# The distance bias of the second stage, written to DRAM in 16 transfers instead of 4, from a tile of its own

## The chip, the cores and the metric

The kernel runs on one core of one Trainium2 chip. Its time is the device time of one execution in microseconds (us); the number that counts is the median of several executions. The engines are TensorE (PE in the profile, its weight loads PEld), VectorE (DVE), ScalarE (ACT), GpSimd (POOL) and SyncE (SP). ACT and SP also issue DMAs: ACTq and SPq are such issues.

## What is computed

The program is one token mixer block with a large expert layer (the first block), followed by two hybrid layers (the second stage), for 256 tokens of width 1024 in float32. Cut to the parts that matter here:

```python
def first_block(...):
    h = rmsnorm(x, g_mix[l]);  proj = h @ w_in[l]
    attn_out = windowed_gqa(q_a, k_a, v_a, attn_sink[l])
    lru_out = bidir_rglru(xc, ...) * jax.nn.gelu(gate_l)
    mem_out = memory_cross_attention(q_m, k_m, v_m)
    g = jax.nn.sigmoid(gates + gate_b[l])
    merged = g0 * (attn_out @ p_attn) + g1 * (lru_out @ p_lru) + g2 * (mem_out @ p_mem)
    x = x + merged @ w_out[l]
    x = x + peer_ffn(rmsnorm(x, g_ffn[l]), ...)

def swa_attention(...):            # in each of the two layers of the second stage
    dist = qi - kj
    bias = rel_bias[t5_bucket(jnp.maximum(dist, 0))]      # 8 heads, a row of 384 distances each
    s = jnp.where(valid, s + bias, -jnp.inf)
```

The bias depends on the distance between two tokens alone. So one row of 384 numbers per head says all of it, and a tile of 128 queries needs that row 128 times, each time shifted by one place.

## The kernel before

**Weights.** All weights lie in DRAM in the order in which they are used, in pieces of 1 MB (16 blocks of 128x128). `Stream._slot` (line 76) loads a piece into one of two `raw` buffers (line 86, issued by SP), and for each half of it, a slot of 8 blocks, ACT writes the high part `whi` (line 90) and DVE the rest `wlo` (line 93). There are three `whi`/`wlo` buffers. Each product is three matmuls (`mm3`, lines 173 to 175; `mm3a`, lines 179 to 181). So a weight piece can be loaded once both slots of the piece two before it have been split.

**The order of the work.** The first block, `block1`, runs its projections one after the other on PE. What is not a projection (convolution, attention heads, the recurrence `lru`) is written as generators, which `add` puts into a list; `tick`, called for every second weight block, steps those that are due. A `yield n` makes a task wait `n * 4` ticks, which is `n * 8` weight blocks. `finish` runs a task to its end at once. The framework's scheduler then sets the order on each engine. Each engine works strictly in its order.

**The bias.** `rel_bias` (line 1428) is such a task, added in line 448. It loads the 32x8 table and a 33x384 one-hot matrix `boh`, multiplies them (line 1438, `prb`), copies the 8x384 result to SBUF (line 1440, `sbb`), and writes that to the DRAM scratch `bias_scr` 128 times, once for each query row, in four transfers of 32 copies (lines 1442 to 1446), issued by ACT. Each transfer reads 8 partitions and writes 8x32 pieces of 384 floats (1536 bytes). `issue_after(ws.on_scalar)` only says that the issue stands behind the latest `whi` on ACT. Each transfer is followed by `yield 2`. `self.finish(t_rel)` stands in line 594, ahead of the gated projections. The scratch is read much later, in the second stage (`bias`, line 1096).

**Tiles that share a place.** `sbb` has the tag `b2`, with three buffers, which it shares with `boh`, with `pts` of the attention (line 666) and with `lth` of the recurrence (line 549). A new tile of a tag waits until the tile three before it has been read by all its readers. For `sbb` the readers are the four transfers.

**What comes after.** The gated projections (`gated`, line 608) are 8 columns each for three branches: `pg` on PE, `gth` on ACT (line 617), `pp` on PE. The recurrence `lru` is finished inside them. Then come the output projection (line 604) and the expert layer, which begins with a transfer of `keys` (line 934, issued by ACT).

Of the kernel before, what the change touches and what calls it, by code (L numbers as in the profile page):

```python
# [7 lines left out]
F32 = mybir.dt.float32  # L8
# [11 lines left out]
P = 128  # L20
# [28 lines left out]
N_WARM = 50  # L49
NORM_AT = (5, 6)  # L50
REL_AT = 20
LOAD_AT = (2, 2, 4, 6, 10, 12, 12, 14, 14)


# [71 lines left out]
def blocks(*tiles):  # L126
    return [t[:, i, :] for t in tiles for i in range(t.shape[1])]


class Core:  # L130
# [285 lines left out]
    def block1(self):  # L416
        tc, nc, a, ws = self.tc, self.nc, self.a, self.ws
        with ExitStack() as st:
# [3 lines left out]
            p = st.enter_context(tc.tile_pool(name="b1", bufs=1))  # L422
# [4 lines left out]
            def T6(dt=F32):  # L427
                return pa.tile([P, 6, S], dt, tag="t6", name="t6", bufs=8)
# [4 lines left out]
            def raw16():  # L433
                b = blocks(T6(F32R), T6(F32R), T6(F32R))
                return [(b[i], b[8 + i]) for i in range(8)]
# [7 lines left out]
            with tc.issue_after(last[0].ins), tc.issue_after(last[1].ins):  # L443
# [3 lines left out]
                self.small1(p)  # L447
            t_rel = self.add(self.rel_bias(p), REL_AT)

# [141 lines left out]
                                          oh[:, h, :], ol[:, h, :]), 2 + 2 * h) for h in range(4)]  # L591


            self.finish(t_rel)
            mg = p.tile([P, KD, S], F32, tag="x8", name="mg", bufs=1)
            gh, gl_ = T8(), T8()
            br = [(0, "p_attn", 6, ah, al, t_att), (2, "p_mem", 4, oh, ol, t_mem), (1, "p_lru", 6, lh, ll, [t_lru])]
# [2 lines left out]
                           self.hgb[:, n * KD:n * KD + KD], b == 0, b == len(br) - 1, ts)  # L600
            self.dump("mg", mg)

            raw = raw16()
            acc = self.residual(("w_out", 0, 0), KD, gh, gl_, raw, self.pc("g_ffn"))
            self.lead(("w_peer_q", 0, 0), raw, self.pc("g_ffn"), [acc], lambda ps: self.rsqrt(ps[:, 0, :]), LEAD_Q)
# [459 lines left out]
    def mixers(self, l):  # L1065
        tc, nc, a, ws = self.tc, self.nc, self.a, self.ws
        with ExitStack() as st:
# [25 lines left out]
            def load(out, in_):  # L1093

                with tc.issue_after(ws.on_scalar):
                    nc.scalar.dma_start(out=out, in_=in_)
                return
                yield
            loads = [[self.add(load(o, i), w) for w, o, i in x] for x in (
                [(LOAD_AT[0], sink, a["swa_sinks"][l].to_broadcast([P, 8]))]  # L1100
                + [(LOAD_AT[1 + i], bias[:, 4 * i:4 * i + 4, :],
                    bass.AP(scr.tensor, scr.offset + 127 + 4 * 384 * i, [[8 * 384 - 1, P], [384, 4], [1, S]]))
                   for i in range(2)],
                [(LOAD_AT[3], cl[:, :L_DEC], a["cstl"][:, :L_DEC])],
                [(LOAD_AT[4], cl[:, L_DEC:], a["cstl"][:, L_DEC:])],
                [(LOAD_AT[5], wst, a["gmlp_wsT"][l]), (LOAD_AT[6], bs, a["gmlp_bs"][l].to_broadcast([P, 512])),
                 (LOAD_AT[7], lng[:, 0, :], a["gmlp_ln_g"][l].to_broadcast([P, 512])),
                 (LOAD_AT[8], lng[:, 1, :], a["gmlp_ln_b"][l].to_broadcast([P, 512]))])]
# [319 lines left out]
    def rel_bias(self, p):  # L1428

        nc, a = self.nc, self.a  # L1430
        rb = p.tile([33, 8], F32, tag="rlb", name="rlb")
        nc.vector.memset(rb, NEG)
        nc.scalar.dma_start(out=rb[0:32, :], in_=a["rel_bias"])
        oh = p.tile([33, 384], F32, tag="b2", name="boh", bufs=3)
        nc.scalar.dma_start(out=oh, in_=a["bucket"])
        self.bias_scr = self.dr.tile([P, 8 * 384], F32, name="bias_scr")
        ps = self.bg.tile([8, 384], F32, tag="bg", name="prb")
        nc.tensor.matmul(ps, lhsT=rb, rhs=oh, start=True, stop=True)
        sb = p.tile([8, 384], F32, tag="b2", name="sbb", bufs=3)
        nc.scalar.activation(out=sb, in_=ps, func=AF.Copy)  # L1440
        scr = self.bias_scr
        for i in range(0, P, 32):
            with self.tc.issue_after(self.ws.on_scalar):
                nc.scalar.dma_start(out=bass.AP(scr.tensor, scr.offset + i * 8 * 384, [[384, 8], [8 * 384, 32], [1, 384]]),
                                    in_=sb[:, None, :].to_broadcast([8, 32, 384]))
            yield 2

    def ffn(self, l):
        tc, nc, a, ws = self.tc, self.nc, self.a, self.ws
# [173 lines left out]
```

## Time and profile before

| | us |
|---|---|
| median of 3 executions | 2127.13 (2122.9 to 2136.53) |
| the profiled execution | 2123.62 |
| its span, first to last instruction | 2121.8 |
| PE busy in the span | 2032.5 (96%) |
| ACT busy in the span | 1164.8 (55%) |

The profile shows one execution. Matmuls overlap in the records, so a row's length is longer than the distance to the next one's start; the distance is what a matmul costs. A row "ACTq ... DMA_DIRECT2D" or "SPq ..." is the issue of a transfer, in which the issuing engine is held; the transfer itself runs on the core's 16 DMA engines, and "landing" is the time from issue to its arrival. An entry "[3.78 <-ACT whi L90]" is idle time of that engine just before the instruction, and what ended it.

### The profile page before, as it was taken

To read this page: it belongs to the slowest core of one execution; us is meant where nothing else is said; L and a number is where in the kernel's file an instruction comes from. 1 tells how busy PE (TensorE), PEld (TensorE's weight loads), DVE (VectorE), ACT (ScalarE), POOL (GpSimd) and SP (SyncE) were. 2 spreads that over 40 slices of the span, in tenths; PEclk is the share of its full clock that TensorE was granted. 3 is DMA by queue.
4 is the path that set the end of the run, shared out by engine and by line. 5 is a ranking of instruction groups with operands and counts; after the bars stand their busy time and mean duration, and the time that the engine had idled before them with its cause. 6 is when DMAs were issued, how large, how long until landed. Compare 5 with 4: busy or idle time off the path is not lost.

```text
span 2121.8 us, 41452 instructions
## 1 busy us (share of the span) xinstructions
PE 2032.5 (96%) x16818; PEld 1974.2 (93%) x16818; DVE 1680.1 (79%) x3308; ACT 1164.8 (55%) x1910; POOL 252.3 (12%) x162
## 2 busy tenths in 40 slices
PE   8978999959999999999999989999999999999999
PEld 7958999959999899999999878999999988999997
DVE  7847669998999999996556998977655898977654
ACT  6648754435555455554446656466545657466543
POOL 2101205844000000000000110210000110200000
PEclk9988999979999999999999999999999999999999
DMA  5443554525445444444555642555555643554554
GB/s 209 147 119 124 181 210 168 179 100 178 173 171 177 151 168 179 177 177 163 197 193 185 217 159 100 185 196 178 208 191 197 236 159 120 187 191 179 199 194 154
DMA packets 56923, 370.01 MB, mean 174 GB/s; under 512 B 6491, under 2 KB 10140, under 8 KB 13468
## 3 DMA queue, kind: packets, MB, share of 16 engines
q1 hardware_dynamic: 50256, 357.06, 46.9%
q10 hardware_dynamic: 6476, 10.31, 1.9%
q8 instruction: 131, 2.15, 0.4%
q14 instruction: 60, 0.49, 0.1%
HBM read 364.73 MB, written 2.62 MB: 173 GB/s over the span
## 4 chain that ended last, share of the span: by engine, by line
PE 81%; DVE 9%; issue 3%; DMA 3%; ACT 3%; POOL 1%; ACTq 0%; SPq 0%; POOLq 0%; DVEq 0%
PE mm L175 6%; PE mm L173 6%; PE mm L174 6%; PE acc L174 5%; PE pu L173 5%; PE acc L175 5%; PE acc L173 5%; PE pu L175 5%; PE pu L174 5%; PE pg L175 3%; PE pg L174 3%; PE pg L173 3%; DVE wlo L93 2%; PE mml L173 2%; PE mml L175 2%
## 5 line engine op out<-in xcount | busy, mean ns | idle before, releaser
L90 ACT ACTIVATE whi<-raw 128x1024 fp32r<-128x1024 f32 x677 | 716.9, 1060 | 764.6 <-PE acc L174 170.3
L93 DVE TENSOR_TENSOR wlo<-raw,whi 128x1024 fp32r<-128x1024 f32 x629 | 778.3, 1238 | 323.6 <-ACT whi L90 320.7
L173 PE MATMUL pu<-hh,whi 128*128 128x256 f32 x1024 | 290.5, 284 | 20.3 <-ACT whi L90 20.3
L175 PE MATMUL pu<-hh,wlo 128*128 128x256 f32 x1024 | 287.0, 280 | 3.1 <-POOL wlo L93 3.1
L174 PE MATMUL pu<-hl,whi 128*128 128x256 f32 x1024 | 286.1, 279 | 0.0
L175 PE MATMUL mm<-hh,wlo 128*128 128x256 f32 x1008 | 280.8, 279 | 5.3 <-DVE wlo L93 5.3
L173 PE MATMUL mm<-hh,whi 128*128 128x256 f32 x1008 | 281.6, 280 | 0.0
L174 PE MATMUL mm<-hl,whi 128*128 128x256 f32 x1008 | 280.3, 278 | 0.0
L174 PE MATMUL acc<-ga,whi 128*128 128x256 f32 x1000 | 267.9, 280 | 4.5 <-DVE ga L187 4.4
L175 PE MATMUL acc<-ga,wlo 128*128 128x256 f32 x1000 | 267.3, 279 | 0.0
L173 PE MATMUL acc<-ga,whi 128*128 128x256 f32 x1000 | 242.5, 281 | 5.0 <-ACT ga L186 5.0
L173 PEld LDWEIGHTS pu<-hh,whi 128*128 128x128 f32 x1024 | 194.7, 190 | 20.5 <-ACT whi L90 20.5
L173 PE MATMUL pg<-hh,whi 128*128 128x256 f32 x704 | 199.5, 283 | 12.3 <-ACT lth L552 11.7
L175 PE MATMUL pg<-hh,wlo 128*128 128x256 f32 x704 | 198.4, 282 | 0.6 <-DVE wlo L93 0.5
L175 PEld LDWEIGHTS pu<-hh,wlo 128*128 128x128 f32 x1024 | 194.3, 190 | 3.8 <-POOL wlo L93 3.8
L174 PE MATMUL pg<-hl,whi 128*128 128x256 f32 x704 | 197.7, 281 | 0.0
L175 PEld LDWEIGHTS mm<-hh,wlo 128*128 128x128 f32 x1008 | 190.3, 189 | 7.8 <-DVE wlo L93 6.7
L174 PEld LDWEIGHTS pu<-hl,whi 128*128 128x128 f32 x1024 | 194.0, 189 | 0.0
L174 PEld LDWEIGHTS acc<-ga,whi 128*128 128x128 f32 x1000 | 188.6, 189 | 5.3 <-DVE ga L187 5.3
L174 PEld LDWEIGHTS mm<-hl,whi 128*128 128x128 f32 x1008 | 190.3, 189 | 1.8 <-issue 1.6
L173 PEld LDWEIGHTS mm<-hh,whi 128*128 128x128 f32 x1008 | 190.6, 189 | 1.0 <-issue 0.8
L175 PEld LDWEIGHTS acc<-ga,wlo 128*128 128x128 f32 x1000 | 188.7, 189 | 0.0
(412 smaller groups left out, 4873.4 us busy)
## 6 DMA issues: line engine op xcount, KB each, us to landing
raw<-in_w SPq DMA_DIRECT2D x336, 1024.0 KB, 4.8
raw<-in_w SPq DMA_DIRECT2D x5, 512.0 KB, 7.6
bias<-bias_scr ACTq DMA_DIRECT2D x4, 512.0 KB, 5.4
bias_scr<-sbb ACTq DMA_DIRECT2D x4, 384.0 KB
cl<-in_cstl ACTq DMA_DIRECT2D x2, 576.0 KB, 7.4
x<-in_xT SPq DMA_DIRECT2D x4, 256.0 KB, 5.8
memt<-in_memT ACTq DMA_DIRECT2D x1, 1024.0 KB, 4.8
keys<-in_keysT ACTq DMA_DIRECT2D x1, 1024.0 KB
```

Of the source, the lines that this page charges most:

```text
L90: self.on_scalar = nc.scalar.activation(out=hi, in_=src, func=AF.Copy).ins
L93: i = eng.tensor_tensor(out=lo, in0=src, in1=hi.bitcast(F32), op=ALU.subtract)
L173: mm(out, lhsT=wh, rhs=xh, start=start, stop=False)
L174: mm(out, lhsT=wh, rhs=xl, start=False, stop=False)
L175: mm(out, lhsT=wl, rhs=xh, start=False, stop=stop)
```

## The change

The task writes `bias_scr` in 16 transfers of 8 copies instead of four of 32, and yields 4 instead of 2 after each. `sbb` gets a tag of its own and so a buffer that no other tile uses. `finish(t_rel)` moves from the place ahead of the gated projections to the place behind them.

```diff
+REL_COPIES, REL_PACE = 8, 4
 ...
-            self.finish(t_rel)
             mg = p.tile([P, KD, S], F32, tag="x8", name="mg", bufs=1)
 ...
                            self.hgb[:, n * KD:n * KD + KD], b == 0, b == len(br) - 1, ts)
             self.dump("mg", mg)
 
+            self.finish(t_rel)
             raw = raw16()
 ...
-        sb = p.tile([8, 384], F32, tag="b2", name="sbb", bufs=3)
+        sb = p.tile([8, 384], F32, tag="sbb", name="sbb")
         nc.scalar.activation(out=sb, in_=ps, func=AF.Copy)
         scr = self.bias_scr
-        for i in range(0, P, 32):
+        n = REL_COPIES
+        for i in range(0, P, n):
             with self.tc.issue_after(self.ws.on_scalar):
-                nc.scalar.dma_start(out=bass.AP(scr.tensor, scr.offset + i * 8 * 384, [[384, 8], [8 * 384, 32], [1, 384]]),
-                                    in_=sb[:, None, :].to_broadcast([8, 32, 384]))
-            yield 2
+                nc.scalar.dma_start(out=bass.AP(scr.tensor, scr.offset + i * 8 * 384, [[384, 8], [8 * 384, n], [1, 384]]),
+                                    in_=sb[:, None, :].to_broadcast([8, n, 384]))
+            yield REL_PACE
```

On PE, DVE, POOL and SP every instruction stands where it stood. On ACT only the transfers to `bias_scr` move. One line is added ahead of all functions, so line numbers after the change are higher by one or two.

ACT's order where the first transfers are issued, right behind the copy of `sbb`, before:

```order
L1440 ACTIVATE sbb<-prb 8x384 [waits PE_49,Activation_49]
L1444 DMA bias_scr<-sbb 8x32x384 [waits Activation_49]
L186 ACTIVATE t_939<-po 128x256 [waits PE_49]
L1444 DMA bias_scr<-sbb 8x32x384 x3
L651 ACT_TABLE_LOAD
L651 ACTIVATE apr,ast<-apr,ast 128x256 [waits DVE_49]
```

and now:

```order
L1441 ACTIVATE sbb<-prb 8x384 [waits PE_49]
L1446 DMA bias_scr<-sbb 8x8x384 [waits Activation_49]
L187 ACTIVATE t_939<-po 128x256 [waits PE_49]
L1446 DMA bias_scr<-sbb 8x8x384 x2
L652 ACT_TABLE_LOAD
L652 ACTIVATE apr,ast<-apr,ast 128x256 [waits DVE_49]
```

Of the four large transfers that stood here together, three small ones are left; the other 13 stand further on.

ACT's order a little later, where the next `lth` tile of the recurrence is written; the names in brackets are semaphores, DMAHW ones those of transfers. Before:

```order
L90 ACTIVATE whi<-raw 128x1024 [waits DMAHW0_49,PE_49]
L186 ACTIVATE t_939<-po 128x256 [waits PE_49]
L667 ACTIVATE pts<-pt 128x512 [waits PE_49]
L550 ACTIVATE lth<-mm,hbr 128x256 [waits DMAHW3_49,DMAHW4_49,DMAHW2_49,DMAHW1_49]
L552 ACTIVATE lth<-mm,hbi 128x256
```

and now:

```order
L91 ACTIVATE whi<-raw 128x1024 [waits DMAHW0_49,PE_49]
L1446 DMA bias_scr<-sbb 8x8x384
L187 ACTIVATE t_939<-po 128x256 [waits PE_49]
L668 ACTIVATE pts<-pt 128x512 [waits DMAHW7_49,PE_49]
L551 ACTIVATE lth<-mm,hbr 128x256
L553 ACTIVATE lth<-mm,hbi 128x256
```

The four DMA waits of `lth` are gone. `pts` takes over a wait that stood four rows further up before, for the load of `boh` (DMAHW7). The fourth of the 16 transfers stands behind the `whi`.

ACT's order at the end of the gated projections, up to the transfer of `keys`, before:

```order
L189 ACTIVATE t_1742<-mg 128x256 [waits DVE_49]
L617 ACTIVATE gth<-pg,hgb 128x256 [waits PE_49]
L90 ACTIVATE whi<-raw 128x1024 [waits PE_49,Activation_49]
L90 ACTIVATE whi<-raw 128x1024 [waits DMAHW1_49,PE_49,Activation_49]
L189 ACTIVATE t_1742<-mg 128x256 [waits DVE_49]
L617 ACTIVATE gth<-pg,hgb 128x256 [waits PE_49]
L90 ACTIVATE whi<-raw 128x1024 [waits PE_49,Activation_49]
L189 ACTIVATE t_1742<-mg 128x256 [waits DVE_49]
L90 ACTIVATE whi<-raw 128x1024 [waits DMAHW2_49,PE_49,Activation_49]
L934 DMA keys<-in_keysT 128x2048 [waits DVE_49]
```

and now:

```order
L190 ACTIVATE t_1741<-mg 128x256 [waits DVE_49]
L1446 DMA bias_scr<-sbb 8x8x384
L1446 DMA bias_scr<-sbb 8x8x384 [waits DMAHW5_49]
L618 ACTIVATE gth<-pg,hgb 128x256 [waits PE_49]
L91 ACTIVATE whi<-raw 128x1024 [waits PE_49,Activation_49]
L91 ACTIVATE whi<-raw 128x1024 [waits DMAHW2_49,PE_49,Activation_49]
L190 ACTIVATE t_1741<-mg 128x256 [waits DVE_49]
L618 ACTIVATE gth<-pg,hgb 128x256 [waits PE_49]
L91 ACTIVATE whi<-raw 128x1024 [waits PE_49,Activation_49]
L190 ACTIVATE t_1741<-mg 128x256 [waits DVE_49]
L91 ACTIVATE whi<-raw 128x1024 [waits DMAHW6_49,PE_49,Activation_49]
L935 DMA keys<-in_keysT 128x2048 [waits DMAHW4_49,DMAHW3_49,DMAHW5_49,DMAHW0_49,DVE_49]
```

The last two transfers stand here, with the one before them just ahead of the first row, so three in all stand together. `keys`, whose buffer lies where the first block's tiles lay, now waits for the latest four transfers.

## Rows read from the trace of the kernel before

**Rows 1.** The page: PE's busy time; the clock in 40 slices of 53 us.

```profile
PE 2032.5 (96%) x16818; PEld 1974.2 (93%) x16818; DVE 1680.1 (79%) x3308; ACT 1164.8 (55%) x1910; POOL 252.3 (12%) x162
...
PEclk9988999979999999999999999999999999999999
```

**Rows 2.** Busy time by stretches: PE, PEld, DVE, ACT, POOL, clock, DMA share, GB/s.

```profile
128.00:136.50 8.50, 8.50 (x40) 6.78 (x38) 3.70 (x10) 0.39 (x2) 0.00 (x0) 1.00 0.59 106
136.50:164.00 27.50, 8.83 (x30) 6.23 (x29) 5.39 (x11) 7.91 (x16) 0.00 (x0) 0.70 0.49 101
164.00:168.00 4.00, 4.00 (x20) 4.00 (x21) 2.83 (x7) 4.00 (x9) 1.04 (x2) 0.53 0.02 4
168.00:180.00 12.00, 12.00 (x102) 11.90 (x101) 9.04 (x22) 11.94 (x24) 1.54 (x2) 1.00 0.34 100
```

**Rows 3.** The waits between 120 and 175 us: total, times, longest.

```profile
ACT lth L550 <- DMA bias_scr<-sbb: 13.5, 1, 13.5
...
PE pg L173 <- ACT lth L552: 11.7, 1, 11.7
...
ACT whi L90 <- DMA raw<-in_w: 6.0, 1, 6.0
...
PE mm L179 <- ACT whi L90: 3.8, 1, 3.8
...
PE po L671 <- ACT pts L667: 3.2, 1, 3.2
```

**Rows 4.** ACT's timeline, 126 to 200 us: start, length, what, idle before.

```profile
128.04 0.30 ACTq L1444 DMA_DIRECT2D bias_scr<-sbb  x1
...
128.41 8.15 ACTq L1444 DMA_DIRECT2D bias_scr<-sbb  x3
136.59 1.28 ACT L651 ACT_TABLE_LOAD   x1 [7.80 <-issue]
...
147.67 1.06 ACT L90 ACTIVATE whi<-raw 128x1024 fp32r<-128x1024 f32 x1 [5.95 <-DMA raw<-in_w]
...
163.03 0.47 ACT L550 ACTIVATE lth<-mm,hbr 128x256 f32<-128x256 f32 x1 [13.54 <-DMA bias_scr<-sbb]
```

**Rows 5.** PE's timeline from 118 to 172 us.

```profile
127.24 1.13 PE L671 MATMUL po<-pts,vt 128*128 128x256 f32 x4
128.20 1.03 PE L642 MATMUL ps<-kt,t 128*128 128x256 f32 x4
...
132.28 0.60 PE L243 MATMUL pt<-cst,apr 128*128 128x128 f32 x4
...
135.94 0.39 PE L180 MATMUL mm<-whi,t 128*128 128x512 f32 x1
136.16 0.40 PE L181 MATMUL mm<-wlo,t 128*128 128x512 f32 x1
...
163.92 0.58 PE L173 MATMUL pg<-hh,whi 128*128 128x256 f32 x1 [11.66 <-ACT lth L552]
```

**Rows 6.** The tile `bias_scr`: lengths of the issues on ACT, in ns, shortest, median, longest.

```profile
L1444 ACTq DMA_DIRECT2D bias_scr<-sbb x4: 297/1838/4414, 128.0 to 132.1; - x4
```

**Rows 7.** Line 86 from 128 to 133 us: the one weight load issued at 128.7.

```profile
DMA to landing us min/median/max: 18.9/18.9/18.9
```

**Rows 8.** Line 86 from 164 to 310 us: the 24 weight loads issued there.

```profile
DMA to landing us min/median/max: 4.7/5.0/6.1
```

**Rows 9.** DMA queues between 131 and 143 us (q10 is ACT's, q1 is SP's).

```profile
q10 hardware_dynamic: 381, 0.57, 44.6%
q1 hardware_dynamic: 54, 0.38, 7.4%
```

**Rows 10.** ACT's timeline, 243 to 330 us.

```profile
254.13 1.06 ACT L90 ACTIVATE whi<-raw 128x1024 fp32r<-128x1024 f32 x1 [2.10 <-DMA raw<-in_w]
...
287.34 1.06 ACT L90 ACTIVATE whi<-raw 128x1024 fp32r<-128x1024 f32 x1 [1.76 <-PE pg L174]
...
298.67 0.36 ACTq L934 DMA_DIRECT2D keys<-in_keysT  x1
```

## The prediction

> **What bounds the kernel now.** I read the page first: PE is busy 96% of the span, so time can come only from where PE stands still or runs at a low clock, and the clock row shows three slices with an 8 or a 7, of which the two 8s lie between 106 and 212 us [rows 1]. Then the stretches in there, around the bias transfers: from 136.5 to 164 us PE is busy 8.8 of 27.5 us, at a mean granted clock of 0.70 of 2.4 GHz, and for 4 us more it runs nearly all at 1.2 GHz (0.53) [rows 2]. That is a hole of some 20 us in a kernel that has few. The list of waits there names what stands before PE: 11.7 us for `lth`, 3.8 us for `whi`, 3.2 us for `pts`, all on ACT; ACT itself waits 13.5 us for the bias transfers and 6.0 us for a weight load [rows 3]. ACT's timeline puts these in a row [rows 4]: the four issues begin at 128.04 and hold ACT to 136.59 (of this 7.80 us is idle for "issue"); a `whi` comes only at 147.67, since its weights are late; and `lth` starts at 163.03, when the last transfer has read `sbb`. So three holds stand one behind the other, all from the same 1.5 MB of small pieces, and removing one alone would leave PE to the next.
>
> **The change part by part.** I work out where PE would be at each step if ACT no longer holds it.
>
> *The issues.* The shortest issue of a 256-piece transfer took 297 ns, the longest 4414 [rows 6], and the first row is the short one [rows 4]: the queue takes some transfers at once, and only the later ones hold ACT. Three transfers of 64 pieces are 192 pieces, less than the first transfer alone, so I take 0.3 us for each. ACT is then free at about 129.1 instead of 136.59. Between the two stand half a softmax and a `whi`, for which PE stopped at 136.4 (136.16 and a matmul [rows 5]) and waited 3.8 us [rows 3], to 140.2, which is 3.6 us after ACT went on. From 129.1 these 3.6 us lead to 132.7, and PE needs it at 136.4. So that wait goes, with over 3 us in hand.
>
> *The weights.* The load issued at 128.7 took 18.9 us [rows 7] where 24 loads later took 4.7 to 6.1 [rows 8]. ACT's queue had 512 pieces ahead of it (two transfers). The price of a piece: 44.6% of 16 engines over 12 us is 85.7 us for 381 pieces, 0.225 us each [rows 9]. 44.6% is about 7 of 16 engines, so a new transfer of 64 pieces takes 64 x 0.225 / 7.1 = 2.0 us; the whole, 35 us from 128.04 to 163.03 over 16, gives 2.2. With two small transfers ahead instead of two large ones the load lands 5 + 4 = 9 us after 128.7, at 138 at the latest, and its `whi` is done by 139.5.
>
> *The wait of `lth`.* It is gone, by ACT's order. In front of it stand that `whi`, a split and a `pts`, so `lth` can start near 140.5.
>
> *PE's own work up to `pg`.* Between 136.16 and 163.92 PE has 12 matmuls of 512 columns, two groups `po`, one `pt`, one `ps` (30 records in all [rows 2]). From rows at full clock [rows 5]: 12 x 0.23 (136.16 less 135.94) = 2.8; 2 x 0.96 (128.20 less 127.24) = 1.9; `pt` 0.60; `ps` 1.03. The sum is 6.3 us, so PE reaches `pg` at 136.4 + 6.3 = 142.7 instead of 163.92. That is 21.2 us. `lth` is done by then, and both `pts` too.
>
> *The clock.* With no hole PE has no reason to fall to 1.2 GHz there. From 164 to 168, 20 matmuls took 4.0 us; the next stretch has 102 in 12.0, 0.118 us each, so 20 cost 2.4 [rows 2]. That is 1.6 us more.
>
> *The 13 transfers that are left.* They carry the same 1.2 MB in the next 150 us. ACT pays up to 0.3 us for each issue, but from 180 on it has idle time; I count 0.3 us in all for the stretch where it is full (168 to 180: 11.94 of 12 [rows 2]), into which one of them falls. The weights pay if such a transfer is ahead of them: 2.0 us on some of the engines, against loads of 5.0 us, two `raw` buffers and a period of 16 blocks x 3 x 0.118 = 5.7 us. How tight that is one row shows: at 254.13 a `whi` waited 2.1 us for its weights [rows 10], and PE, which has no row of waiting there, did not notice. So 2 us are covered by the slots that are already split; I cost the 13 at 0.5 us together. If that cover were gone they would cost 13 x 2.0 = 26 us. They cannot gain. The last three stand together: 6 us of DMA time from about 288.5 (behind the `whi` at 287.34), ended near 297 even behind a load in flight. `keys`, the one new wait, was issued at 298.67 [rows 10], with `whi` instructions behind it; I cost it at nothing, and it costs what the transfers are later than that.
>
> The sum: 21.2 + 1.6 - 0.3 - 0.5 = 22.0 us. The profiled execution took 2123.62 (span 2121.8 and 1.8 around it), so 2101.6; it lies 3.5 us under the median of 2127.13, and the three runs spread over 13.6, so I forecast **2102**, 1.2% under the median. One per cent is about what a measurement of this kernel can tell from no change, and here it is 21.3 us: the forecast is close to that line.
>
> *A rule against it.* That a load goes behind what was issued before it, and not beside it, I take from a row: while the load of 128.7 waited, SP's queue moved 54 packets in 12 us, ACT's 381 [rows 9]. The Trainium skill says otherwise ("DMA: Bandwidth & Descriptors", section "Queues, rings and completion order"): an engine with work on several queue rows takes turns between them, a packet from each. By that rule the load would not have stood behind 512 pieces, and the trace does not agree here. What it would do to the late transfers is the second rival.
>
> **The rivals.**
>
> *A hold remains behind the first.* The wait of `lth` goes, but ACT is held in front of it all the same, because the weights of 128.7 are as late as before: 18.9 us [rows 7] and not 9, 10 us more. For it: three waits in one chain, and only one is taken out by the new place alone. Against it: the issue and the piece count go down by a factor of four. Gain 22 - 10 = 12: **2111.6**. Chance 0.16.
>
> *Late transfers share turns with the loads.* Then a transfer delays also a load that was issued before it, so that nearly each of the 13 meets one. Between no cost and the whole 2.0 us I take 1.0 each, 13 us: 22.0 + 0.5 - 13 = 9.5, so **2114**. For it: a `whi` was late even without them [rows 10]. Against it: PE did not wait then, and [rows 9]. Chance 0.13.
>
> *Each late transfer stops PE.* The other side: one mechanism, a `whi` too late by a whole transfer each time, and after each stop a stretch at 1.2 GHz as after the hole. Price 2.0 + 1.6 = 3.6 us each, 13 of them 47: 2123.6 - 22.8 + 47 = **2148**. It decides for slower by 1% from (22.8 + 21.3) / 13 = 3.4 us for each transfer. Against it: the cover above, and a half-clock stretch that came after a stop of 11.7 us, not of 2. Chance 0.04.
>
> *The spread is not one.* ACT's order has three transfers together at either end, so the small size may do little and the new place all of it; at the start three small ones are still only 6 us of DMA time, so the time is **2104**. Chance 0.05.
>
> **How the numbers follow.** The forecast has 0.62. It and the last rival lie under 2105.9, 1% below the median, apart from the share that the spread of the runs carries over it: faster 0.61. The first two rivals and that share are within 1%: 0.35. Slower 0.04. The range goes down to 2096 (no cost for the late transfers, runs 4 us below the forecast) and up to 2115, over the first two rivals; the 26 us of the upper bound stay outside with the third.
>
> **What would show it.** In the changed profile: the `lth` row has no wait for `bias_scr`; the first three issues last about 0.3 us each and ACT goes on at about 129; the load issued near 128.7 lands in under 10 us; `pg` of the first gated column starts near 143 at a granted clock of 1.00; from there to the expert layer PE's rows stay as far apart as before. Wrong would be: a PE wait over 3 us between 130 and 150; `whi` rows ended by `raw` several times between 160 and 280 with PE waits behind them; `keys` held and a `whi` late after it; or a `pg` on time and the end of the program not 20 us earlier.

## The result and the profile after

The changed kernel takes 2101.68 us, the median of 4 runs (2100.12 to 2103.45), and the kernel before, run beside it, 2125.02 (4 runs, 2117.86 to 2136.53). The ratio is 0.989, with a 95% interval of 0.9865 to 0.9915: faster by 23.3 us, 1.1%. Forecast were 2102 us and a range of 2096 to 2115. The profiled execution took 2103.45 us (span 2101.7).

The page of the changed kernel, the rows that answer to [rows 1]:

```profile
PE 2026.5 (96%) x16818; PEld 1969.1 (94%) x16818; DVE 1681.7 (80%) x3308; ACT 1164.1 (55%) x1910; POOL 254.8 (12%) x162
...
PEclk9999999979999999999999999999999999999999
```

The two slices at 8 in the clock row are gone, and the 7 further on is still there. PE did the same 16818 instructions in 6.0 us less busy time: those in and behind the hole no longer run at the low clock, and the distance between matmuls, which differs from one execution to the next (last experiment), is in this number too. The two profiled spans lie 20.1 us apart (2121.8 less 2101.7), so 14.1 us are time in which PE stood still.

The stretches around the first transfers (stretch, sum, PE, PEld, DVE, ACT, POOL, granted clock, DMA share, GB/s), which answer to [rows 2]:

```profile
128.00:136.50 8.50, 8.50 (x39) 6.36 (x38) 6.22 (x17) 6.56 (x15) 1.27 (x1) 1.00 0.50 145
136.50:142.00 5.50, 5.50 (x28) 4.57 (x27) 3.63 (x4) 3.60 (x7) 0.00 (x0) 1.00 0.51 123
142.00:164.00 22.00, 22.00 (x173) 21.39 (x172) 17.37 (x37) 21.29 (x42) 3.90 (x5) 1.00 0.42 136
```

PE is busy in every microsecond from 128 to 164, at a granted clock of 1.00. Before, it was busy 8.8 us of the last 27.5 of these, at a mean clock of 0.70. The other place to look at is ACT's column in the first row: 6.56 us busy where it had 0.39, because the issues no longer hold it.

ACT's timeline of the changed kernel, 126 to 150 us (start, length, what, idle before), which answers to [rows 4]:

```profile
130.05 0.30 ACTq L1446 DMA_DIRECT2D bias_scr<-sbb  x1
...
130.42 1.67 ACTq L1446 DMA_DIRECT2D bias_scr<-sbb  x2
132.12 1.28 ACT L652 ACT_TABLE_LOAD   x1 [1.32 <-issue]
...
138.53 1.06 ACT L91 ACTIVATE whi<-raw 128x1024 fp32r<-128x1024 f32 x1 [1.05 <-DMA raw<-in_w]
...
141.31 0.47 ACT L551 ACTIVATE lth<-mm,hbr 128x256 f32<-128x256 f32 x1
```

Read it against [rows 4] row by row. This profile runs 2.0 us later than that of before already at the first issue (130.05 against 128.04), so I compare distances from there. From the first issue to the table load it was 8.55 us and is now 2.07; to the late `whi` 19.63, now 8.48; to `lth` 34.99, now 11.26. The wait of `lth` for `bias_scr` is gone from its row, and the wait of `whi` for its weights has shrunk from 5.95 us to 1.05.

The same place on PE, which answers to [rows 5]:

```profile
139.32 1.02 PE L672 MATMUL po<-pts,vt 128*128 128x256 f32 x4
...
142.47 1.02 PE L672 MATMUL po<-pts,vt 128*128 128x256 f32 x4
143.33 1.03 PE L643 MATMUL ps<-t,t 128*128 128x256 f32 x4
144.00 0.47 PE L174 MATMUL pg<-hh,whi 128*128 128x256 f32 x1
```

No row carries a wait. The first `pg` starts 13.95 us after the first issue (144.00 less 130.05), where it was 35.88 (163.92 less 128.04). That is 21.9 us of the gain in one distance. I use this distance, from the first issue to the first `pg`, for the experiments too, and call it D.

The end of the block is the second place. The output projection's first matmul, before and in the changed kernel:

```profile
295.68 0.28 PE L173 MATMUL mml<-t,whi 128*128 128x256 f32 x1
```

```profile
271.01 0.28 PE L174 MATMUL mml<-t,whi 128*128 128x256 f32 x1
```

From `pg` to `mml` it is 131.76 us before and 127.01 after, 4.8 less. That is more than the 1.6 us that I had for the clock, and what makes the difference comes with the last experiment.

### The profile page after: what moved, and what is told of

Its sections match the earlier page's. It is cut to its first block, busy times and chain, and to the rows that moved or that the text cites. A ratio compares the mean times of both kernels' runs of the same rounds, so it can differ in the third digit from the quotient of the medians.

```text
span 2101.7 us, 41465 instructions
## 1 busy us (share of the span) xinstructions
PE 2026.5 (96%) x16818; PEld 1969.1 (94%) x16818; DVE 1681.7 (80%) x3308; ACT 1164.1 (55%) x1910; POOL 254.8 (12%) x162
## 4 chain that ended last, share of the span: by engine, by line
PE 82%; DVE 8%; ACT 4%; issue 3%; DMA 2%; POOL 1%; ACTq 0%; SPq 0%; POOLq 0%; DVEq 0%
PE mm L176 6%; PE mm L175 6%; PE mm L174 6%; PE acc L175 6%; PE acc L174 5%; PE acc L176 5%; PE pu L174 5%; PE pu L175 5%; PE pu L176 5%; PE pg L176 3%; PE pg L174 3%; PE pg L175 3%; DVE wlo L94 2%; PE mm L182 2%; PE mm L180 2%
```

## The experiments

The theory is the prediction's: PE's hole came from three holds one behind the other (the issues, the late weights, the wait of `lth`), so taking one away leaves PE to the next, and the late transfers are covered. The rivals say that one part did it all, or that the late transfers cost something.

The first four kernels below were run beside 25 runs of the kernel before, with a median of 2126.92 us, and the last three beside 17, with 2123.45. Their ratios are to these.

**The place alone.** The kernel before, with a buffer of its own for `sbb` and nothing else:

```diff
-        sb = p.tile([8, 384], F32, tag="b2", name="sbb", bufs=3)
+        sb = p.tile([8, 384], F32, tag="sbb", name="sbb")
```

> The kernel before with one edit: sbb gets a place of its own; the four large transfers stay together. Measured by the distance D from the first bias transfer's issue to the first gated pg on TensorE: 35.9 us before (128.04 to 163.92), 13.95 after (130.05 to 144.00). Theory of three holds in a chain: the issue still holds ACT for 8 us and the weight load still lands after about 18 us, only the 11.7 us that pg waited for lth go, so D is about 24, and the time about 12 us under before, 2113. Rival, the shared place was all of it: D about 14 and the time about 2102.

Measured: 2117.21 us (10 runs, 2112.88 to 2125.51), ratio 0.9954 [0.9938, 0.9971]. ACT's timeline of this kernel, 126 to 166 us:

```profile
127.52 0.30 ACTq L1444 DMA_DIRECT2D bias_scr<-sbb  x1
...
127.88 8.14 ACTq L1444 DMA_DIRECT2D bias_scr<-sbb  x3
136.06 1.28 ACT L651 ACT_TABLE_LOAD   x1 [7.81 <-issue]
...
147.32 1.06 ACT L90 ACTIVATE whi<-raw 128x1024 fp32r<-128x1024 f32 x1 [6.13 <-DMA raw<-in_w]
```

And PE's waits in it, 124 to 350 us:

```profile
PE mm L179 <- ACT whi L90: 4.0, 1, 4.0
PE po L671 <- ACT pts L667: 3.7, 1, 3.7
```

The first two holds stand as they did in [rows 4], to a quarter of a microsecond: 7.81 us of issue, 6.13 us for the weights, whose load took 19.1 us from issue to landing (18.9 in [rows 7]). Only `pg`'s wait of 11.7 us in [rows 3] has gone. D is 24.61, which is 11.3 less than before, and `pg` to `mml` is 131.98, the same in sum as before (with more and other PE waits in it, and from 240 us on a shorter distance between matmuls). The time lies 4 us above the 2113 that I expected. So the place alone is worth about half of D's gain; the other half stands on the two holds that are left.

**Everything but the small size.** The changed kernel with four transfers of 32 copies, spread 16 apart:

```diff
-REL_COPIES, REL_PACE = 8, 4
+REL_COPIES, REL_PACE = 32, 16
```

> The changed kernel with four transfers of 32 copies and a yield of 16, so the same bytes over the same stretch in four lumps. Theory that a load goes behind what was issued before it and that the slots cover 2 to 3 us: the first load lands in about 12 us instead of 7.4, D about 16; later lumps of some 7 us come ahead of a load two or three times and cost TensorE about 3 us each; the time is 2107 to 2111. Rival, spreading is what counts and the size of a transfer does nothing: D about 14, time 2102, no waits of TensorE over 1 us in the gated stretch.

Measured: 2116.13 us (10 runs, 2108.78 to 2119.41), ratio 0.9948 [0.9932, 0.9964], slower than either side of my forecast for it. At the start it went as I had thought: ACT has one issue, of 0.30 us, no hold, and the load of 129.7, with 256 pieces ahead of it, landed 11.1 us after its issue. D is 15.35, only 1.4 over the changed kernel. The loss is further on. ACT there, around the second transfer:

```profile
156.31 0.28 ACTq L1446 DMA_DIRECT2D bias_scr<-sbb  x1
...
168.43 1.06 ACT L91 ACTIVATE whi<-raw 128x1024 fp32r<-128x1024 f32 x1 [5.61 <-DMA raw<-in_w]
```

and PE behind it:

```profile
169.91 0.38 PE L174 MATMUL mm<-t,whi 128*128 128x256 f32 x1 [2.30 <-ACT gth L618]
...
178.39 0.30 PE L244 MATMUL pt<-cst,apr 128*128 128x128 f32 x1 [3.85 <-DVE apr L660]
```

The load of 157.71 was issued behind 256 pieces, its `whi` waited 5.6 us, and this time PE had no cover: it stood for 2.3 and 3.9 us. The second of these two stops is in the kernel before and in the changed one too, 1.4 to 1.5 us long, as the last experiment shows; only what is above that can be the transfer's. The stretch had a mean clock of 0.89:

```profile
170.00:185.00 15.00, 10.93 (x69) 10.09 (x70) 12.42 (x31) 13.79 (x27) 2.52 (x3) 0.89 0.22 76
```

The third transfer (217.92) cost time as well: the `whi` at 231.34 waited 4.60 us for its weights, and PE stood behind it:

```profile
234.24 0.39 PE L174 MATMUL pg<-hh,whi 128*128 128x256 f32 x1 [2.11 <-ACT gth L618]
```

From `pg` to `mml` this kernel takes 137.91 us, some 8 more than the changed kernel does in its second profile (below). So the size matters a second time: a large transfer that is spread takes its hold along, to a place where PE has less in hand. The same run also has the test of the order of service. The load of 216.37 was issued 1.55 us before the third lump (217.92), the load of 220.45 behind it. The DMA queues in the first microseconds of the lump, 217.9 to 220.4 (packets, MB, share of 16 engines; q1 is SP's, q10 ACT's):

```profile
q1 hardware_dynamic: 114, 0.92, 88.7%
q10 hardware_dynamic: 5, 0.01, 0.8%
```

and from 220.9 to 226.5:

```profile
q10 hardware_dynamic: 188, 0.29, 47.0%
q1 hardware_dynamic: 72, 0.52, 27.1%
```

SP's load goes first and lands after 4.9 us, as if the lump were not there; then the lump has the larger share (188 packets to 72), and the load behind it comes late. In the stretch 133.6 to 143 of the kernel before, it is the lump that came first:

```profile
q10 hardware_dynamic: 299, 0.45, 44.4%
q1 hardware_dynamic: 4, 0.03, 0.8%
```

In these two stretches what was issued first was served first. It is not the whole of it: behind the third lump 72 packets of SP's load went beside the lump's 188, whose packets took 47.0% of the 16 engines' time. Which engines a load's packets go to, no row shows.

**The end of the wait put back.** The changed kernel with `finish(t_rel)` ahead of the gated projections again:

```diff
+            self.finish(t_rel)
             mg = p.tile([P, KD, S], F32, tag="x8", name="mg", bufs=1)
 ...
-            self.finish(t_rel)
             raw = raw16()
```

> The changed kernel with the finish of the bias task back ahead of the gated projections; small transfers and the place of its own stay. On ACT 14 of 16 transfers then stand close behind the first, ten of them with a wait for an earlier transfer's semaphore. Theory: the bytes ahead of the loads are as many as before and ACT is held by the transfers it waits for, so D is 25 to 36 and the time 2113 to 2126. Rival, small size and own place do the work and the later finish nothing: D under 18, time under 2106.

Measured: 2121.36 us (10 runs, 2110.41 to 2126.09), ratio 0.9971 [0.9953, 0.9989]. ACT's timeline of it, from 139 us:

```profile
139.33 7.08 ACTq L1446 DMA_DIRECT2D bias_scr<-sbb  x4
146.46 1.06 ACT L91 ACTIVATE whi<-raw 128x1024 fp32r<-128x1024 f32 x1 [6.09 <-issue]
146.48 7.45 ACTq L1446 DMA_DIRECT2D bias_scr<-sbb  x3
153.97 0.38 ACT L187 ACTIVATE t<-po 128x256 fp32r<-128x256 f32 x1 [6.46 <-issue]
```

and PE:

```profile
156.65 2.08 PE L672 MATMUL po<-pts,vt 128*128 128x256 f32 x4 [15.35 <-ACT pts L668]
```

`finish` issues every transfer that is left at the place where it stands, so the 13 come within 30 us, and they hold ACT as the large ones did, seven of them for 14.5 us. PE waits 15.4 us, D is 31.15. Of the 21.9 us this kernel has 4.7. The later `finish` is therefore the part without which the other two give little: it is what lets the transfers spread.

**One transfer in place of 16.** The changed kernel, with the other 15 left out; the later read of the bias is turned to what this one has written, so that every query row gets the same bias and the output is another:

```diff
-        for i in range(0, P, n):
+        for i in range(0, n, n):
 ...
-                    bass.AP(scr.tensor, scr.offset + 127 + 4 * 384 * i, [[8 * 384 - 1, P], [384, 4], [1, S]]))
+                    bass.AP(scr.tensor, scr.offset + 127 + 4 * 384 * i, [[0, P], [384, 4], [1, S]]))
```

> The changed kernel with only the first of the 16 transfers; the other 120 copies are left out, and every query row reads the first row's bias. What 15 transfers still cost in the changed kernel. Theory: TensorE waited 0.9 us there in all behind late weights, so the time is within 2 us of the changed kernel and D is 13 to 14, while the waits of ACT for weights (five, 11.6 us) fall to one or two. Rival, every transfer costs TensorE about 1 us by sharing the engines: the time is about 12 us lower, 2090.

Measured: 2098.48 us (4 runs, 2096.33 to 2103.67), ratio 0.9878 [0.9851, 0.9906], against 0.989 and, run again, 0.9898 for the changed kernel. The intervals lie over each other: 15 transfers cost 3 to 4 us by the ratios, and by the intervals perhaps nothing; the rival's 12 us are out. D is 13.94, the same as with all 16. So no time of the first stop is left to gain: some 13.9 is PE's own work. What the transfers do cost shows on ACT. Its wait for weights from 124 to 330 us in this kernel,

```profile
ACT whi L91 <- DMA raw<-in_w: 4.4, 3, 1.9
```

in three waits where I expected one or two, is less than the changed kernel has between 180 and 290 us alone:

```profile
ACT whi L91 <- DMA raw<-in_w: 11.6, 5, 3.3
```

In its second profile (below) the changed kernel has 5.8 us there, in four waits, and 7.5 from 124 to 330, so this wait too differs between executions.

**Eight and 32 transfers.** The changed kernel with other sizes at the same pace of copies:

```diff
-REL_COPIES, REL_PACE = 8, 4
+REL_COPIES, REL_PACE = 16, 8
```

> The changed kernel with eight transfers of 16 copies and a yield of 8: the size between the changed kernel's and the four lumps, over the same stretch. With four lumps the distance D from the first transfer to pg came out 1.6 us longer than in the changed kernel and the lump in the recurrence stretch cost TensorE some 7 us. Theory that only what a lump takes beyond the cover of the split slots costs time: lumps of half the size (3 to 4 us) cost 0 to 2 us each where they come ahead of a load, D 14 to 15, the time 2102 to 2108. Rival, any transfer above the small size throws the recurrence out of step: 2112 or more.

```diff
-REL_COPIES, REL_PACE = 8, 4
+REL_COPIES, REL_PACE = 4, 2
```

> The changed kernel with 32 transfers of 4 copies and a yield of 2: the same bytes in half the size, with twice the issues, 13 of them with a wait for an earlier transfer's semaphore, and six more together at the end. Theory that the changed kernel has nothing left to give here: D 14, the time within 4 us of the changed kernel, 2098 to 2106. Rival, issues on ScalarE cost what the DMA engines don't: 16 more issues of 0.3 us and their waits show in the full stretch, 5 us or more slower, 2107 and up.

Measured: 2110.58 us for eight (10 runs, 2104.17 to 2129.28), ratio 0.9938 [0.9909, 0.9966], and 2100.24 for 32 (4 runs, 2090.88 to 2116.87), ratio 0.9889 [0.9831, 0.9947]. Eight fell between what the theory and its rival gave, so its time alone decides nothing, but its trace does. Its D is 15.35, as with four, and for one reason: two transfers of 128 pieces stand ahead of the first load where one of 256 stood, and it is the pieces ahead that count. What its profile loses up to `mml` beyond that is 3.6 us, nearly all at one wait on PE, the second of the four-transfer kernel's:

```profile
PE pt L244 <- DVE apr L660: 3.7, 1, 3.7
```

The changed kernel waits 1.44 us there in the profile that this is held against (the last experiment), and behind the longer stop the clock is low for longer (0.77 from 170 to 185 us against 0.89). D and this make up 5.2 of the 8.3 us between the two medians; where the rest is, I do not know. From 180 us to `mml` PE waits for nothing in this kernel, though five more transfers of 128 pieces fall there: this size costs where ACT is full (9.96 of 10 us from 150 to 160), not in the stretch behind it.

With 32 transfers D is 13.95, and the time can't be told from that of 16. The wait of `whi` for weights does not fall further with the size (13.1 us in 8 waits from 124 to 330 us, where the changed kernel has 14.8 in 7 and 7.5 in 5 in its two profiles).

**The changed kernel again.** The same program, beside these two:

> The changed kernel as it is, once more beside the others, with five rounds. Both theories of the late transfers say the same here: 2102, D about 14.0. It tells how far two executions of one program differ: the matmuls of 256 columns stood 0.113 us apart in some stretches and 0.118 in others, at a granted clock of 1.00; if that is a drift of the chip and not of the kernel, the stretches lie elsewhere in this profile, and from 212 to 300 us TensorE makes 356 or 342 matmuls in 40 us without a change in the program.

Measured: 2102.29 us (6 runs, 2097.89 to 2110.43), ratio 0.9898 [0.9861, 0.9936]. D is 13.74. Its stretch from 260 to 300 us, and that of the first profile of the same program:

```profile
260.00:300.00 40.00, 40.00 (x342) 40.00 (x342) 29.07 (x48) 24.19 (x38) 0.61 (x1) 1.00 0.62 221
```

```profile
260.00:300.00 40.00, 40.00 (x356) 40.00 (x354) 29.18 (x48) 24.96 (x39) 0.61 (x1) 1.00 0.67 232
```

Both are full, both have a granted clock of 1.00, and yet one has 356 matmuls in 40 us and the other 342: 0.112 and 0.117 us each. The profile of before has 342 too:

```profile
260.00:300.00 40.00, 40.00 (x342) 40.00 (x341) 26.27 (x39) 20.93 (x31) 0.61 (x1) 1.00 0.54 187
```

There is a second difference, in the clock. In all three profiles PE stops for about 1.4 us at the same `pt`, first before, then the first and the second profile of the changed kernel:

```profile
194.21 0.30 PE L243 MATMUL pt<-cst,apr 128*128 128x128 f32 x1 [1.42 <-DVE apr L659]
```

```profile
172.53 0.30 PE L244 MATMUL pt<-cst,apr 128*128 128x128 f32 x1 [1.50 <-DVE apr L660]
```

```profile
170.24 0.30 PE L244 MATMUL pt<-cst,apr 128*128 128x128 f32 x1 [1.44 <-DVE apr L660]
```

Behind this stop the granted clock is low before, 1.00 in the first profile of the changed kernel, where PE waited as long, and low again in the second (stretches in the same order):

```profile
194.00:200.00 6.00, 5.56 (x29) 5.04 (x30) 5.84 (x15) 5.98 (x15) 1.14 (x2) 0.72 0.28 116
```

```profile
170.00:185.00 15.00, 13.19 (x104) 12.42 (x103) 12.13 (x29) 14.94 (x30) 2.52 (x3) 1.00 0.42 147
```

```profile
170.00:185.00 15.00, 14.53 (x100) 13.84 (x101) 12.11 (x25) 13.20 (x24) 2.48 (x3) 0.89 0.33 131
```

The same 50 matmuls with this stop among them take, from start to start, 9.86 us before, 8.39 in the first profile and 9.88 in the second: 1.5 us for the clock. So the `pg` to `mml` distance of the first profile (127.01) is not to be compared with that of before; that of the second is, which has the same low stretch and the same distance between matmuls: its `pg` starts at 141.78 and its `mml` at 271.71.

```profile
271.71 0.28 PE L174 MATMUL mml<-t,whi 128*128 128x256 f32 x1
```

That is 129.93 us, 1.8 less than the 131.76 of before.

The two profiles differ over the rest of the span as well. The second starts its first bias transfer at 128.04, as before does, is 22.1 us ahead of before at the first `pg`, 24.0 at `mml` and 24.4 at the end (span 2097.4). The first is 24.7 ahead at `mml` and only 20.1 at the end. Most of what it loses goes in the last 180 us, where it has the longer distance between matmuls and before has the shorter. 40 us of that stretch, before and then the first profile of the changed kernel:

```profile
2000.00:2040.00 40.00, 40.00 (x355) 40.00 (x354) 22.60 (x31) 20.25 (x30) 0.00 (x0) 1.00 0.52 187
```

```profile
1980.00:2020.00 40.00, 40.00 (x342) 40.00 (x341) 21.84 (x28) 19.33 (x29) 0.00 (x0) 1.00 0.51 188
```

So single profiles of one program lie some 4 us apart here for reasons that are not the change's.

No version here that does the whole work is ahead of the changed kernel by more than the intervals. In a table, with D and the distance from `pg` to `mml`:

| kernel | us | ratio | D | `pg` to `mml` |
|---|---|---|---|---|
| before | 2125.02 | 1 | 35.88 | 131.76 |
| place alone | 2117.21 | 0.9954 | 24.61 | 131.98 |
| finish early | 2121.36 | 0.9971 | 31.15 | 127.85 |
| four, spread | 2116.13 | 0.9948 | 15.35 | 137.91 |
| eight, spread | 2110.58 | 0.9938 | 15.35 | 133.54 |
| the change, 16 | 2101.68 | 0.9890 | 13.95 | 127.01 |
| the change, again | 2102.29 | 0.9898 | 13.74 | 129.93 |
| 32, spread | 2100.24 | 0.9889 | 13.95 | 125.73 |
| one transfer | 2098.48 | 0.9878 | 13.94 | 128.70 |

## Why the prediction was right

*The chain of three holds.* It was right that they stand one behind the other, and that taking one away leaves the next. The place alone brought 11.3 of 21.9 us in D, and the place and the small size without the late `finish` 4.7. The rival "the spread is not one" is thereby out in its own words: the place does not do all. The rival "a hold remains" described, by its gain of 12 us, what the place alone does (11.3), not the change.

*The issues.* The step was right in what it led to and wrong in its number. I took 0.3 us for each of the three; the first took 0.30, the other two 1.67 together, as the changed kernel's row of the tile shows (shortest, median, longest in ns):

```profile
L1446 ACTq DMA_DIRECT2D bias_scr<-sbb x16: 270/271/1351, 130.1 to 263.7; - x16
```

So ACT was free 2.07 us after the first issue and not 1.1. The argument that 192 pieces are fewer than the first large transfer alone does not hold for how long an issue lasts: the third issue was held although less lay ahead of it. Over 3 us were in hand, and PE did not notice.

*The weights.* Forecast was a landing at most 9 us after issue. `whi` started 7.8 us after it (138.53 less 130.7), with 128 pieces ahead; with 256 ahead the load took 11.1 us, with 512 18.9 and 19.1. About 2 us for 64 pieces, as I had it, gives 5 + 8 = 13 and 5 + 16 = 21 for these, some 2 us too much each.

*PE's own work.* From the first issue to `pg` I forecast 14.7 us (142.7 less 128.04), and measured 13.95, 13.94 and 13.95 in three kernels, and 13.74 in the changed kernel's second profile. The gain of the step was 21.9 us against 21.2.

*The clock.* 1.6 us forecast, 1.8 measured, as the two distances from `pg` to `mml` at the same distance between matmuls. At the first `pg` the granted clock is 1.00. What I had overlooked is the second low stretch, behind the stop of 1.42 us at 194.21: the change neither removes it nor brings it, and it came in one of the two profiles of the changed kernel. My argument against the third rival, that a half-clock stretch had come after a stop of 11.7 us and not of 2, was therefore wrong; one came after 1.4.

*The late transfers.* I costed them at 0.8 us. The distance from `pg` to `mml` in the second profile has no room for any: it is shorter than before by the clock's 1.8. But the mechanism was not the one I gave. I had said that the cover of the split slots holds, with one late `whi` in [rows 10] to show how tight. In the changed kernel's first profile ACT waits for weights five times between 180 and 290 us, for 1.7 to 3.3 us each; two of them:

```profile
215.62 1.06 ACT L91 ACTIVATE whi<-raw 128x1024 fp32r<-128x1024 f32 x1 [2.40 <-DMA raw<-in_w]
...
275.93 1.06 ACT L91 ACTIVATE whi<-raw 128x1024 fp32r<-128x1024 f32 x1 [3.31 <-DMA raw<-in_w]
```

while PE's waits there are two (and none in the second profile):

```profile
PE pg L176 <- DVE wlo L94: 0.6, 1, 0.6
...
PE pg L174 <- ACT gth L618: 0.3, 1, 0.3
```

Half of what I had named as the sign of a wrong forecast was there (`whi` rows ended by `raw` several times), and the other half, PE waits behind them, was 0.9 us in all. The longest of these waits for weights, 3.3 us, put none on PE; 4.6 and 5.6 us, after lumps of 256 pieces, did. How much is covered depends on the place: with eight transfers the `whi` that led to the longer `pt` stop (163.38) had waited 2.95. That also bounds the rival by which each late transfer stops PE: true for some of the larger ones, not for these.

*`keys`.* Costed at nothing. Its row follows the last of these `whi` rows at once, at 276.40, so what it waited for was done by then.

*The rule of turns.* The Trainium skill ("DMA: Bandwidth & Descriptors", section "Queues, rings and completion order") has an engine alternate between its queue rows, a packet from each. The trace does not agree, counted in its own packets: 299 of ACT's queue against 4 of SP's where the lump came first, 114 of SP's against 5 where the load did. So the second rival (2114), which rested on such turns, is out by the second of these and by the time. Whether the order is set in the queues or ahead of them, where the pieces are made, no run here shows.

*The sum.* 22.0 forecast; 21.9 + 1.8 = 23.7 by these two steps, 24.4 between the spans of before and of the changed kernel's second profile, 20.1 with its first, and 23.3 in the medians. That the median came out within half a microsecond of the forecast is partly luck: I had taken the sum from the profiled execution, which lay 3.5 us under the median shown then, and the later runs of before had a median 2 us lower than that.

## What to carry to other kernels

Where a wait, an issue and a late load come from one burst of small transfers, look for all three on the timeline before taking one away: here the buffer alone gave half, and spreading the burst gave the other half only once the point that collects it had moved too. What a burst costs the loads behind it goes by the pieces already in line, not by the number of transfers. A spread transfer is free while the wait that it puts on the next load stays within what the engine behind it has in hand, so cut it until that is so (128 pieces here at the first stop, 64 where ACT is full), and no further: 32 transfers gave nothing over 16.

## What was not expected of the hardware

The third issue of only 64 pieces held ACT for 1.35 us, while one of 256 pieces with nothing ahead took 0.30, and the last three of the changed kernel, which stand together at 263.00, took 1.05 us in all; no row shows what makes the difference. A stop of 1.4 us was followed by the low clock in one execution and not in another. And matmuls of one program stood 0.117 us apart in one profile and 0.112 in another, over 40 us without a gap and at a granted clock of 1.00 in both; no row of the profile shows why. Left open beside these is how one late `whi` makes the stop at `pt` longer by 2.4 us in the four-transfer kernel. Of the three parts only the place was taken by itself. Neither the small size alone nor the later `finish` alone was run, so what either gives from the shared place is not shown.
